# Hybrid encoder layer on one core: the mixer's value projection in 2x2 blocks, behind the block of keys and value gates

## The chip, the cores and the metric

The kernel runs on one core of a Trainium2 chip. The metric is the device time of one execution in microseconds (us), as the median of several runs. The engines are named as in the profile: PE (matrix products) with PEld (loading of its weights), DVE (vector), ACT (scalar), POOL (GpSimd) and SP (which issues most loads).

## The reference, cut to what matters

The layer is a half-step FFN, a mixer with two head groups, and a second half-step FFN, each between two norms. Width is 2048, 256 tokens, float32. What the change touches is the mixer's input projection:

```python
h = rms_norm(x, pre_norm_mix[layer])
q_h, i_h, f_fwd, f_bwd, g_h, q_a, k_a, v_a = jnp.split(h @ w_mix_in[layer], split_at, axis=-1)
y_h = hgrn2_mixer(q_h, i_h, f_fwd, f_bwd, g_h, lb_fwd_all[layer], lb_bwd_all[layer],
                  hgrn_out_norm[layer])
y_a = window_attention(q_a, k_a, v_a, attn_sink[layer], rel_bias_table)
mixed = jnp.concatenate([y_h.astype(x.dtype), y_a.astype(x.dtype)], axis=-1) @ w_mix_out[layer]
```

The columns 1024 to 2047 of `w_mix_in` give `i_h`, the values of the recurrent heads (in the kernel: `vh`). The columns 6144 to 6655 give `k_a` and `v_a`, the keys and values of the attention heads (in the kernel: `kz` and `va`). Each is a product of 256 tokens x 2048 inputs with 2048 inputs x 1024 or 512 columns.

## The kernel before, in words

**Precision.** Every product is made of three. An operand is split into a high part and a low part: ACT casts it (line 177, `h`), and DVE subtracts the cast from it (line 178, `l`). PE then adds high x high, high x low and low x high into one PSUM bank. Weights arrive by SP in chunks of 128 x 2048 (1 MB, three raw buffers), and each chunk is split in two halves of 1024 columns into h and l buffers, five of each. `xt` holds the transposed input, 16 blocks of 128 inputs, high and low, with the two halves of the tokens side by side; two neighbouring blocks are a pair, so there are eight pairs.

**A projection by 512 columns** (`proj_N`, lines 367 to 393) goes through the 16 blocks of inputs and for each half of the tokens issues three products of 128 x 512: 96 products in all, into two banks. `LeadN` (line 345) makes the first half of such a projection inside the end of the first FFN.

**The order of the mixer's start.** The values' first 512 columns, of which blocks 0 to 7 are done by `LeadN` during the FFN's last steps and blocks 8 to 15 after it; the second 512 columns; then the 512 columns of keys and gates; then the head projections (`headpair`, by `proj_T_pieces`, lines 311 to 343), whose products are lines 322 and 327. Meanwhile ACT makes the squares for the norm, POOL the power -0.5 and DVE copies the scale of each half of the tokens to `rs2` (line 264). The results are scaled on the way out of PSUM by `rs2`. `spread` (line 284) broadcasts a factor per token along the partitions, by one product on PE, into `R`; the head projections are scaled by `R`.

**Blocks with seven products.** The class `Blocks` (lines 415 to 607) is used by the FFNs and by the output projection, not by the input projection. It takes a pair of input blocks and two banks of 512 columns for each half of the tokens, a 2x2 by 2x2 block product. A plain pair takes eight block products (24 on PE). A pair that has prepared sums of `xt` (its entry in `sums`) takes seven (21 on PE), by sums on both sides. `seven` (line 476) prepares the weights of such a pair on DVE and ACT:

```python
split_act(*first, b11)
nc.vector.tensor_tensor(
    four[:, 0:2], four[:, 0::3], four[:, 1:2].to_broadcast([P, 2, 512]), ALU.add
)
lower = split_half(raw, 1)
nc.vector.tensor_tensor(b22, b11, b22, ALU.add)
upper = split_half(raw, 0)
nc.vector.tensor_tensor(b21, b22, b21, ALU.add)
last = split_half(raw, 1)
```

`products` (line 498) issues the seven on PE. Four of them go to banks of their own, and `fold` (line 526) adds these on DVE into the four result banks: four additions for the mixed sums (lines 535, 536, 539, 542) and one into each bank (548, 552, 556, 558). `play` (line 589) issues a plain pair; at the first plain pair behind the last one with sums it puts the steps of the fold between the products, and the products of the later pair add to the same banks. `sums_of` (line 406) makes the sums of `xt`: one operation of 256 columns and two of 128.

Since sums across the two halves of the tokens are only right with one scale, the first input projection of an FFN first multiplies the second half of the tokens in `xt` by the ratio of the two scales' powers of two: `power_and_rest` (line 266) makes `ratio` and `rest` in six small operations, `spread(ratio, 1)` broadcasts it, and `even` (line 1073) scales a pair (128 x 512). The results are then scaled by `rest`.

**Order.** The mixer's instructions are not in an order written by hand. A planner gives each engine its order before the run, from its own estimate of durations: of what is ready it takes what stands earliest in the program. An instruction that waits for a buffer or a result can be overtaken by later ones in the planner's order; on the chip each engine then keeps that order. The FFNs' inner parts are issued in program order (`manual_schedule`).

Of the kernel before, what the change touches and what calls it, by code (L numbers as in the profile page):

```python
# [11 lines left out]
F32 = mybir.dt.float32  # L12
F32R = mybir.dt.float32r
# [4 lines left out]
ALU = mybir.AluOpType  # L18
AX = mybir.AxisListType

P = 128
D = 2048
T = 256
DFF = 5632
KT = D // P
# [12 lines left out]
def hymba_layer_kernel(  # L38
# [25 lines left out]
    nc = tc.nc  # L64
# [11 lines left out]
    def nm(s):  # L76
        uid[0] += 1
        return f"{s}_{uid[0]}"

    def pa():  # L80
        return psum.tile([P, 512], F32, tag="pa", name=nm("pa"))
# [55 lines left out]
    R = const.tile([P, T], F32, tag="R", name="R")  # L137
# [38 lines left out]
    def split_act(hi, lo, src):  # L176
        nc.scalar.copy(hi, src)  # L177
        nc.vector.tensor_tensor(lo, src, hi.bitcast(F32), ALU.subtract)  # L178
# [62 lines left out]
    def pre_stats():  # L241
        with tc.issue_after(last["act"].ins):
            pre_stats_now()
# [22 lines left out]
    def power_and_rest():  # L266

        for part, a, b in ((two, 0x7F800000, 0), (rest, 0x007FFFFF, 0x3F800000)):
            nc.vector.tensor_scalar(
                part.bitcast(I32), rs2.bitcast(I32), a, b, ALU.bitwise_and, ALU.bitwise_or  # L270
            )
        nc.vector.tensor_scalar(
            ratio.bitcast(I32),
            two[:, 0:1].bitcast(I32),
            0x7F800000,
            0x7F800000,
            ALU.bitwise_and,
            ALU.bitwise_xor,
        )
        nc.vector.tensor_scalar(ratio, ratio, two[:, 1:2], 0.5, ALU.mult, ALU.mult)  # L280
        nc.vector.tensor_scalar(rest[:, 1:2], rest[:, 1:2], two[:, 0:1], None, ALU.mult)
        nc.vector.tensor_copy(rest[:, 0:1], rs2[:, 0:1])

    def spread(factor=rs2, n=2):

        ps = pb()
        for m in range(n):
            nc.vector.tensor_scalar(
                R[:, m * P : (m + 1) * P], ident, factor[:, m : m + 1], None, ALU.mult
            )  # L290
        nc.tensor.matmul(ps[:, : n * P], ones, R[:, : n * P], start=True, stop=True)
        nc.vector.tensor_copy(R[:, : n * P], ps[:, : n * P])
# [86 lines left out]
    def proj_N(*a, **kw):  # L379
        for _ in proj_N_pieces(*a, **kw):  # L380
            pass

    def proj_N_pieces(w, c0, n, xt, slot, k0=0):

        kn = 2048 // n
        half = kn // 2
        for kc in range(k0 // kn, KT // kn):
            hs, ls = split_load(source_N(w, c0, n, kc))
            for m in range(2):
                for kk in range(kn):  # L390
# [218 lines left out]
    class Pairs(Blocks):  # L609
# [26 lines left out]
        def source(self, u):  # L636
            return Pairs.part(self.w, u, self.now)
# [12 lines left out]
        def left_sums(self, u):  # L650
            if self.ready and u in self.ready:
                return self.ready.pop(u)
            if u in self.kept:
                return self.kept[u]
            keep = self.now == 0 and u in self.keep
            if keep and u in self.near:
                w = self.room.tile([P, 4, 2, P], F32R, tag="sp", name=nm("sp"), bufs=3)
            else:
                tag = f"sp{u}" if keep else "sp"
                w = far["pool"].tile([P, 4, 2, P], F32R, tag=tag, name=nm("sp"), bufs=1 if keep else 2)  # L660
            split_act(w[:, :, 0, :], w[:, :, 1, :], self.sums[u])
            if keep:
                self.kept[u] = w
            return w
# [240 lines left out]
    def pair_of(xt, u):  # L905
        return xt[u // 4][:, u % 4 * 2 : u % 4 * 2 + 2]

    class Gated(Blocks):


# [127 lines left out]
    def ffn(gated, w_dn, post_gain, again, gain=None, lead=None, aside=None):  # L1038

        with ExitStack() as st:  # L1040
# [31 lines left out]

            def even(u):

                x = gated.tiles[u].rearrange("p k i t -> p (k i) t")[:, :, P:T]
                nc.vector.tensor_tensor(
                    x, x.bitcast(F32), R[:, None, 0:P].to_broadcast([P, 4, P]), ALU.mult
                )

            def sums_in(u):  # L1080
                x = gated.tiles[u].bitcast(F32)
# [428 lines left out]
    def again_from(src):  # L1510
# [4 lines left out]

        return again

    vbanks = [pa(), pa()]
    xt = ffn(
        gated,  # L1520
        w_ffn1_down[0],
        post_norm_ffn1,
        again_from(x[0]),
        gain=lambda: later["cols"][:, 0:16],
        lead=LeadN(w_mix_in[0], 1024, vbanks),
        aside=other_vectors,
    )
    cols = later["cols"]
# [3 lines left out]
    with ExitStack() as s2:  # L1532
# [21 lines left out]
        def lower_bounds():  # L1554
            l0, l1 = cols[:, 32:48], cols[:, 48:64]
            nc.vector.tensor_tensor(lbm, l0, l1, ALU.max)
            nc.vector.tensor_tensor(e0, l0, lbm, ALU.subtract)
            nc.vector.tensor_tensor(e1, l1, lbm, ALU.subtract)
            nc.scalar.activation(e0, e0, AF.Exp)
            nc.scalar.activation(e1, e1, AF.Exp)  # L1560
            nc.vector.tensor_tensor(e1, e0, e1, ALU.add)
            nc.vector.reciprocal(e1, e1)
            nc.vector.tensor_tensor(lb, e0, e1, ALU.mult)
            nc.vector.tensor_scalar(oml, lb, -1.0, 1.0, ALU.mult, ALU.add)

        w_in = w_mix_in[0]
        vh = mid.tile([P, 2, 1024], F32, tag="vh", name="vh")
        for cg in range(2):
            sl = [pa(), pa()] if cg else vbanks
            if cg == 0:  # L1570
                pre_stats()
                with tc.issue_after(last["rs2"].ins):
                    lower_bounds()
            proj_N(w_in, 1024 + cg * 512, 512, xt, sl, k0=0 if cg else 8)
            for m in range(2):
                nc.scalar.mul(
                    vh[:, m, cg * 512 : (cg + 1) * 512], sl[m], rs2[:, m : m + 1]
                )


# [35 lines left out]
            return z  # L1616


        sl = [pa(), pa()]
        for i, _ in enumerate(proj_N_pieces(w_in, 6144, 512, xt, sl)):  # L1620
            if i == 16:
                spread()
        va = mid.tile([P, 2, 256], F32, tag="va", name="va")
        kz = mid.tile([P, 2, 256], F32, tag="q", name="kz")
        for m in range(2):
            nc.scalar.mul(kz[:, m, :], sl[m][:, :256], rs2[:, m : m + 1])
            nc.scalar.mul(va[:, m, :], sl[m][:, 256:], rs2[:, m : m + 1])
        kT = mid.tile([P, 2, T], F32, tag="kT", name="kT")

        def turned_keys():  # L1630
# [129 lines left out]
        def gates(half):  # L1760

            sl = [pa(), pa()]
            for _ in proj_N_pieces(w_in, 4096 + half * 512, 512, xt, sl):
                side_step()
            g = mid.tile([P, 2, 512], F32, tag="g", name=nm("g"))
            for m in range(2):
                by = rs2[:, m : m + 1]
                nc.scalar.activation(g[:, m, :], sl[m], AF.Sigmoid, scale=by)
                nc.vector.scalar_tensor_tensor(g[:, m, :], sl[m], by, g[:, m, :], ALU.mult, ALU.mult)
            return g  # L1770
# [246 lines left out]
```

## Time and profile before

| | us |
|---|---|
| median of 3 runs | 1822.63 (1822.04 to 1824.23) |
| the profiled execution's own time | 1824.3 |
| its span in the profile | 1822.5 |
| mean granted PE clock of the profiled execution | 0.999 |

The profile is of one execution. Rows of windows give a stretch of the span, its length, the busy time of each engine in it with the number of rows in brackets, the granted PE clock, the mean share of the DMA engines and GB/s. Rows of groups give line, engine, operation, output <- inputs, shape and count, then busy time and the mean duration in ns, then idle time of the engine in front of them with what ended it. Rows in order of time give start, duration, engine, line and operation, with idle time and its cause in brackets. Times of rows are us from the start of the span.

### The profile page before, as it was taken

Reading aid. Unit: us, or ns where it says so; the run is one execution under the profiler, and the core shown is the slowest. Engines: PE = TensorE matmul, PEld = TensorE weight load, DVE = VectorE, ACT = ScalarE, POOL = GpSimd, SP = SyncE. Lnnn points to the kernel's source line nnn. Section 1 sums busy time; section 2 is a strip of 40 time slices with the busy share of each in tenths; the row PEclk is TensorE's granted clock in tenths of the full one; section 3 lists DMA queues with packets and bytes.
Section 4 is the critical chain, followed back from the end, with each engine's and each line's share of the span. In section 5 each row is a group of like instructions: output and inputs, shape, how many; then the busy total and the mean of one; then the engine's idle time right before and its main releaser. Section 6 shows DMA issues by size and latency. Waiting matters only on the chain.

```text
span 1822.5 us, 23466 instructions
## 1 busy us (share of the span) xinstructions
PE 1808.9 (99%) x8420; PEld 1502.0 (82%) x8420; DVE 1605.0 (88%) x2073; ACT 1137.1 (62%) x1508; POOL 162.9 (9%) x155
## 2 busy tenths in 40 slices
PE   9999999999999999999999999999999999999998
PEld 7888888888888888888888888888888888888886
DVE  7999999999989989477687798899999999998986
ACT  7565666666666657476587556556666666566653
POOL 1011111111011100000000000111111111011110
PEclk9999999999999999999999999999999999999999
DMA  8889999998698995655454456889999999699894
GB/s 303 240 235 284 278 281 257 250 261 247 224 343 263 300 300 191 196 183 176 162 174 150 162 208 243 253 242 266 283 271 269 256 248 252 195 339 302 274 303 160
DMA packets 212052, 447.59 MB, mean 246 GB/s; under 512 B 11752, under 2 KB 46656, under 8 KB 211168
## 3 DMA queue, kind: packets, MB, share of 16 engines
q1 hardware_dynamic: 180032, 385.14, 60.7%
q0 software_dynamic: 31904, 60.96, 19.5%
q8 instruction: 66, 1.08, 0.2%
q14 instruction: 50, 0.41, 0.1%
HBM read 433.46 MB, written 12.60 MB: 245 GB/s over the span
## 4 chain that ended last, share of the span: by engine, by line
PE 86%; DVE 7%; ACT 3%; DMA 2%; issue 2%; POOL 0%; DVEq 0%; ACTq 0%; SPq 0%; POOLq 0%
PE pa L454 37%; PE pb L454 32%; PE pa L322 5%; DVE l L178 4%; PE pa L327 3%; PE pa L377 2%; PE pa L375 2%; PE pa L376 2%; DMA raw<-in_w_ffn_down_dram 2%; ACT h L177 1%; PE pa L1131 1%; PE pb L1131 1%; DMA raw<-in_w_ffn_gate_up_dram 0%; DVE la L178 0%; PE pb L1738 0%
## 5 line engine op out<-in xcount | busy, mean ns | idle before, releaser
L177 ACT CAST h<-raw 128x1024 fp32r<-128x1024 f32 (+1 forms) x867 | 854.8, 1013 | 465.3 <-PE pb L454 152.9
L178 DVE TENSOR_TENSOR l<-raw,h 128x1024 fp32r<-128x1024 f32 (+1 forms) x867 | 987.8, 1170 | 134.4 <-ACT h L177 100.6
L454 PE MATMUL pa<-h,xt 128*128 128x512 f32 x1096 | 384.9, 392 | 0.1
L454 PE MATMUL pb<-h,xt 128*128 128x512 f32 x940 | 336.7, 392 | 0.3 <-DVE pb L1188 0.3
L454 PEld LDWEIGHTS pa<-h,xt 128*128 128x128 f32 x1096 | 206.0, 188 | 44.2 <-DVE xt L233 0.6
L454 PE MATMUL pa<-l,xt 128*128 128x512 f32 x548 | 214.0, 391 | 0.0
L454 PEld LDWEIGHTS pb<-h,xt 128*128 128x128 f32 x940 | 176.5, 188 | 42.5 <-DVE pb L1195 3.6
L454 PE MATMUL pb<-l,xt 128*128 128x512 f32 x470 | 183.3, 390 | 0.0
L967 POOL DMA_DIRECT2D raw<-in_w_ffn_gate_up_dram x78 | 94.6, 1212 | 733.8 <-DVE l L178 665.8
L454 PE MATMUL pb<-h,ht 128*128 128x512 f32 x452 | 159.2, 389 | 0.0
L454 PE MATMUL pa<-h,ht 128*128 128x512 f32 x452 | 159.1, 389 | 0.0
L322 PE MATMUL pa<-xt,h 128*128 128x512 f32 x512 | 124.5, 393 | 0.2 <-ACT h L177 0.2
L454 PEld LDWEIGHTS pa<-l,xt 128*128 128x128 f32 x548 | 103.2, 188 | 20.6 <-DVE l L178 0.8
L454 PE MATMUL pa<-h,xs 128*128 128x512 f32 x312 | 111.6, 389 | 0.0
L322 PEld LDWEIGHTS pa<-xt,h 128*128 128x128 f32 x512 | 93.8, 188 | 18.7 <-ACT h L177 0.6
L454 PE MATMUL pb<-h,xs 128*128 128x512 f32 x312 | 108.7, 389 | 0.0
L454 PEld LDWEIGHTS pb<-l,xt 128*128 128x128 f32 x470 | 88.3, 188 | 16.8
L454 PEld LDWEIGHTS pb<-h,ht 128*128 128x128 f32 x452 | 84.8, 188 | 17.6
L454 PEld LDWEIGHTS pa<-h,ht 128*128 128x128 f32 x452 | 84.9, 188 | 17.5
L454 PE MATMUL pa<-l,ht 128*128 128x512 f32 x226 | 88.2, 390 | 0.9 <-DVE l L178 0.9
L454 PE MATMUL pb<-l,ht 128*128 128x512 f32 x226 | 87.9, 389 | 0.0
L1273 POOL DMA_DIRECT2D raw<-in_w_ffn_down_dram x38 | 46.0, 1212 | 374.2 <-DVE la L178 337.2
(292 smaller groups left out, 2575.6 us busy)
## 6 DMA issues: line engine op xcount, KB each, us to landing
raw<-in_w_ffn_gate_up_dram SPq DMA_DIRECT2D x350, 512.0 KB, 5.9
raw<-in_w_ffn_down_dram SPq DMA_DIRECT2D x88, 1024.0 KB, 7.8
raw<-in_w_mix_in_dram SPq DMA_DIRECT2D x52, 1024.0 KB, 5.0
raw<-in_w_ffn_gate_up_dram POOLq DMA_DIRECT2D x78, 512.0 KB, 8.1
raw<-in_w_ffn_down_dram POOLq DMA_DIRECT2D x38, 512.0 KB, 10.1
raw<-in_w_mix_out_dram SPq DMA_DIRECT2D x16, 1024.0 KB, 5.0
ht<-away SPq DMA_DIRECT2D x24, 512.0 KB, 10.3
away<-ht SPq DMA_DIRECT2D x16, 512.0 KB, 7.0
```

What stands on the lines that cost most here:

```text
L177: nc.scalar.copy(hi, src)
L178: nc.vector.tensor_tensor(lo, src, hi.bitcast(F32), ALU.subtract)
L322: nc.tensor.matmul(slot[f], weights(hs, kk, f), xcol(xt, k), start=(k == 0), stop=(k == KT - 1))
L327: nc.tensor.matmul(slot[f][:, 0:T], weights(ls, kk, f), xcol(xt, kh * 8 + kk, 0), start=False, stop=False,)
L375: nc.tensor.matmul(dst, xh, h[:, o : o + n], start=(k == 0), stop=False)
L376: nc.tensor.matmul(dst, xh, l[:, o : o + n], start=False, stop=False)
L377: nc.tensor.matmul(dst, xl, h[:, o : o + n], start=False, stop=(k == KT - 1))
L454: nc.tensor.matmul(self.bank(at), lhs, rhs, start=(n == 1), stop=n in (ends, self.of[at]), skip_group_check=n > ends,)
L967: nc.gpsimd.dma_start(raw[:, 0:1024].rearrange("p (k c) -> p k c", k=2), self.source(u, g)[:, :, 1], accum_op=ALU.add,)
L1131: nc.tensor.transpose(bank[:, o : o + P], zs[m][:, k * P : (k + 1) * P], ident)
L1273: nc.gpsimd.dma_start(raws[i][:, 0:1024].rearrange("p (k c) -> p k c", k=2), Pairs.part(w_dn, u, r)[:, :, 512:1024], accum_op=ALU.add,)
```

## The change

The block of keys and gates takes the place of the values' first 512 columns in `LeadN` and is projected first. Then all 1024 value columns are projected at once as `Blocks` (a new subclass `Values`): pairs 0, 1, 3, 6 and 7 plain, pairs 2, 4 and 5 with seven products. For that the second half of the tokens of `xt` is scaled by `ratio` in all eight pairs (`even_half`, the old body of `even` as a function), the sums of pairs 2, 4 and 5 are made (`value_sums`), and what comes after is scaled by `rest`: the values, the gates, and the head projections through `R`. The keys and gates themselves are scaled by `rs2`. The old projection of keys and gates behind the values, with `spread()` in it, is gone.

```diff
+    def even_half(x):
+
+        x = x.rearrange("p k i t -> p (k i) t")[:, :, P:T]
+        nc.vector.tensor_tensor(
+            x, x.bitcast(F32), R[:, None, 0:P].to_broadcast([P, 4, P]), ALU.mult
+        )
+
...
-    vbanks = [pa(), pa()]
+    kvbanks = [pa(), pa()]
...
-        lead=LeadN(w_mix_in[0], 1024, vbanks),
+        lead=LeadN(w_mix_in[0], 6144, kvbanks),
...
-        for cg in range(2):
-            sl = [pa(), pa()] if cg else vbanks
-            if cg == 0:
-                pre_stats()
-                with tc.issue_after(last["rs2"].ins):
-                    lower_bounds()
-            proj_N(w_in, 1024 + cg * 512, 512, xt, sl, k0=0 if cg else 8)
-            for m in range(2):
+        pre_stats()
+        with tc.issue_after(last["rs2"].ins):
+            lower_bounds()
+        power_and_rest()
+
+        class Values(Blocks):
+
+
+            def source(self, u):
+                return Pairs.part(w_in, u, 1)
+
+            def left_sums(self, u):
+                return self.sums[u]
+
+            def folded(self):
+                return [
+                    [y[:, n, :] for n in range(2)]
+                    for y in (
+                        keepy.tile([P, 2, 512], F32, tag=f"yt{4 + m}", name=nm("y"), bufs=1)
+                        for m in range(2)
+                    )
+                ]
+
+        def value_sums(u):
+
+            z, s = (keepy.tile([P, 4, P], F32, tag=f"sy{i}", name=nm("vs"), bufs=1) for i in range(2))
+            x = pair_of(xt, u).bitcast(F32)
+            whole = z.rearrange("p j t -> p (j t)").rearrange("p (k t) -> p k t", k=2)
+            nc.vector.tensor_tensor(whole, x[:, :, 0, :], x[:, :, 1, :], ALU.add)
+            w = keepy.tile([P, 4, 2, P], F32R, tag=f"yt{VALUES.index(u)}", name=nm("xs"), bufs=1)
+            split_act(w[:, :, 0, :], w[:, :, 1, :], sums_of(whole, s))
+            values.sums[u] = w
+
+        VALUES = (2, 4, 5)
+        values = Values({u: pair_of(xt, u) for u in range(KT // 2)}, dict.fromkeys(VALUES))
+        for i, _ in enumerate(proj_N_pieces(w_in, 6144, 512, xt, kvbanks, k0=8)):
+            if i == 2:
+                spread(ratio, 1)
+                for u in range(4):
+                    even_half(pair_of(xt, u))
+                value_sums(2)
+            if i == 7:
+                even_half(pair_of(xt, 4))
+                even_half(pair_of(xt, 5))
+        even_half(pair_of(xt, 6))
+        even_half(pair_of(xt, 7))
+        value_sums(4)
+        va = mid.tile([P, 2, 256], F32, tag="va", name="va")
+        kz = mid.tile([P, 2, 256], F32, tag="q", name="kz")
+        for m in range(2):
+            nc.scalar.mul(kz[:, m, :], kvbanks[m][:, :256], rs2[:, m : m + 1])
+            nc.scalar.mul(va[:, m, :], kvbanks[m][:, 256:], rs2[:, m : m + 1])
+        values.begin(range(KT // 2))
+        values.work(2)
+        value_sums(5)
+        values.work(3)
+        spread(rest)
+        values.work(KT // 2)
+        for m in range(2):
+            for n in range(2):
                 nc.scalar.mul(
-                    vh[:, m, cg * 512 : (cg + 1) * 512], sl[m], rs2[:, m : m + 1]
+                    vh[:, m, n * 512 : (n + 1) * 512], values.c[m][n], rest[:, m : m + 1]
                 )
...
-        sl = [pa(), pa()]
-        for i, _ in enumerate(proj_N_pieces(w_in, 6144, 512, xt, sl)):
-            if i == 16:
-                spread()
-        va = mid.tile([P, 2, 256], F32, tag="va", name="va")
-        kz = mid.tile([P, 2, 256], F32, tag="q", name="kz")
-        for m in range(2):
-            nc.scalar.mul(kz[:, m, :], sl[m][:, :256], rs2[:, m : m + 1])
-            nc.scalar.mul(va[:, m, :], sl[m][:, 256:], rs2[:, m : m + 1])
...
-                by = rs2[:, m : m + 1]
+                by = rest[:, m : m + 1]
```

More of the change, by code (lines that the diff above doesn't have):

```diff
@@ L1073, in even @@
             def even(u):
[L1075 to L1078, printed above, removed]
+                even_half(gated.tiles[u])
             def sums_in(u):
```

## The prediction

> **What bounds the kernel now.** I read the page's totals and its chain first, then the stretch that the change touches, by windows, by groups and in order of time.
>
> ```profile
> PE 1808.9 (99%) x8420; PEld 1502.0 (82%) x8420; DVE 1605.0 (88%) x2073; ACT 1137.1 (62%) x1508; POOL 162.9 (9%) x155
> PE 86%; DVE 7%; ACT 3%; DMA 2%; issue 2%; POOL 0%; DVEq 0%; ACTq 0%; SPq 0%; POOLq 0%
> 718.70:729.60 10.90, 10.90 (x49) 9.01 (x48) 9.49 (x26) 9.63 (x21) 1.10 (x2) 1.00 0.87 282
> 729.60:773.50 43.90, 43.90 (x195) 36.36 (x194) 20.50 (x21) 20.49 (x22) 0.00 (x0) 1.00 0.61 198
> L375 PE MATMUL pa<-h,xt 128*128 128x512 f32 x64 | 25.1, 392 | 0.0
> L376 PE MATMUL pa<-l,xt 128*128 128x512 f32 x64 | 24.9, 389 | 0.0
> L377 PE MATMUL pa<-h,xt 128*128 128x512 f32 x64 | 24.9, 389 | 0.0
> L178 DVE TENSOR_TENSOR l<-raw,h 128x1024 fp32r<-128x1024 f32 x17 | 20.7, 1225 | 23.3 <-ACT h L177 22.7
> L177 ACT CAST h<-raw 128x1024 fp32r<-128x1024 f32 x17 | 17.8, 1052 | 19.5 <-PE pa L377 19.5
> ```
>
> The window rows give length, then busy time of PE, weight loads, DVE, ACT and POOL, the granted clock, the DMA share and GB/s. PE carries 86% of the chain, so a product saved counts fully where PE is the engine that is late. The second window is the stretch in question: from 729.6 us (the first 512 value columns are done) to 773.5 (the second value block and the block of keys and value gates are done). There 192 products of 128x512 run without a gap. Their listed 0.39 us overlap; the step is (43.9 - 0.43 for one broadcast) / 192 = 0.226 us. DVE is busy 20.5 of 43.9 us and waits for ACT's casts, which wait for PE to give back h buffers: the weights are always ready early. But one window earlier DVE is busy 9.5 of 10.9 us. DVE has room only inside the second window, 23.4 us of it, and the change spends it.
>
> **The change on PE.** The three 512-column blocks need 288 products, the new form 96 + 5 x 24 + 3 x 21 = 279. Keys and gates take the first place, half of it inside the FFN's end as before, so 729.6 stays the start and 183 products follow instead of 192. That is 9 x 0.226 = 2.0 us saved. One broadcast becomes two:
>
> ```profile
> 726.10 1.23 DVE L178 TENSOR_TENSOR l<-raw,h 128x1024 fp32r<-128x1024 f32 x1 [0.21 <-ACT h L177]
> 762.88 0.43 PE pb L291 x2
> 1143.96 0.15 DVE L264 COPY scales<-r 128x1 f32<-128x1 f32 x1 [0.73 <-POOL r L187]
> 1145.86 0.29 DVE L288 TENSOR_SCALAR R<-ident,scales 128x128 f32<-128x128 f32 x1
> 1153.11 0.29 DVE L292 COPY R<-pb 128x128 f32<-128x128 f32 x1
> 1153.43 2.50 DVE L1076 TENSOR_TENSOR xt<-xt,R 128x512 fp32r<-128x512 f32 x4
> 731.26 2.36 DVE L178 TENSOR_TENSOR l<-raw,h 128x1024 fp32r<-128x1024 f32 x2 [1.14 <-ACT h L177]
> 764.46 0.42 DVE L292 COPY R<-pb 128x256 f32<-128x256 f32 x1
> 728.05 0.15 DVE L264 COPY scales<-r 128x1 f32<-128x1 f32 x1 [0.47 <-POOL r L187]
> 728.12 0.17 DVE L1556 TENSOR_TENSOR lbm<-cols 128x16 f32<-128x16 f32 x1
> ...
> 729.94 0.18 DVE L1564 TENSOR_SCALAR oml<-lb 128x16 f32<-128x16 f32 x1
> ```
>
> The second row is the broadcast of two halves; the new one has one half, 0.2 us. PE's net gain is 1.8 us, and that is all the change can gain: the stretch has no PE gap that could vanish.
>
> [...]
>
> **The change on DVE.** Durations overlap here too. Four scalings by R (L1076) take 2.50 us, and one takes 0.69, so the step is (2.50 - 0.69)/3 = 0.60 us for 512 columns; two splits take 2.36 with 1.22 for one, so 1.14 for 1024. The same in smaller sizes: 256 columns listed at 0.42 step 0.34, 128 columns listed at 0.29 step 0.20 (estimates, the list value less the same 0.08).
>
> ```profile
> 1157.05 0.42 DVE L408 TENSOR_TENSOR s<-z 128x256 f32<-128x256 f32 x1
> L411 DVE TENSOR_TENSOR sums<-sums,z 128x128 f32<-128x128 f32 x16 | 4.7, 292 | 0.5
> L1083 DVE TENSOR_TENSOR z<-xt 128x512 f32<-128x512 f32 x8 | 5.5, 684 | 0.0
> L178 DVE TENSOR_TENSOR xs<-s,xs 128x512 fp32r<-128x512 f32 x8 | 5.5, 687 | 2.3 <-ACT xs L177 2.2
> L486 DVE TENSOR_TENSOR raw<-raw 128x1024 f32<-128x1024 f32 x4 | 4.9, 1219 | 0.0
> L490 DVE TENSOR_TENSOR raw<-raw 128x512 f32<-128x512 f32 x4 | 2.8, 688 | 0.1
> L548 DVE TENSOR_TENSOR pa<-pa,y 128x512 f32<-128x512 f32 x6 | 4.1, 688 | 0.0
> ```
>
> All new operations stand in the trace of other stages. Counted from 728.05, where the second half's scale lands and the ratio can first be made:
> - power_and_rest, six small operations: from 1143.96 to 1145.86 with one split of 1.14 between, so 0.7 us; lower_bounds as before, seven of 0.17 to 0.25 between its two rows above, about 1.1.
> - spread(ratio): 0.2 for the factor (L288) and 0.2 for the copy (L292); spread(rest): two factors and the copy of both halves, 0.9, as before.
> - even_half, eight times 0.60: 4.8.
> - value_sums, three times 0.60 + 0.34 + 0.20 + 0.20 + 0.60: 5.8.
> - plain pairs 1, 3, 6, 7, two splits each: 8 x 1.14 = 9.1. Pair 0 is split before 728, as the chunk in its place was (the row at 726.10).
> - seven-product pairs 2, 4, 5: a first block 0.60, the double sum (L486) 1.14, two sums 1.20, three splits 3.42, so 6.36 each: 19.1. A plain pair costs 2.28. Three products of 0.226 saved on PE cost 4.1 us of DVE.
> - the fold, eight additions (L535 to L558, one of them shown): 4.8.
>
> The sum is 46.7 us. Where the added time goes: DVE had 20.5 us of work in the stretch and gets about 45 in it.
>
> **What is late next.** DVE takes what stands earlier in the program and is ready. It can begin even_half at about 730.9 (an estimate: 728.1, then 0.7 for power_and_rest, 0.2 for the factor, some 1.3 for the products already under way and the broadcast on PE, 0.2 for the copy, and the hand-overs). The eight even_half and the opening of value_sums(2), 6.2 us, stand ahead of pair 1's splits, so its first low part is there at 738.2; PE, with pair 0 alone (24 x 0.226 and the broadcast from 729.6), runs dry at 735.2. That is 3.0 us idle. The planner can pull pair 3's and later pair 6's products into later gaps, as they need no sums, but not further: every one needs DVE's splits, and the first block of each seven-product pair already waits on DVE. So the end is DVE's queue. Pair 7 comes last: its splits stand behind the last splits of pair 5 and the fold, and its products behind the fold's additions to the same banks. DVE waits itself for the pass of R, for ACT's casts and for the copy that opens the fold:
>
> ```profile
> 1049.20 1.23 DVE L178 TENSOR_TENSOR l<-raw,h 128x1024 fp32r<-128x1024 f32 x1 [0.22 <-ACT h L177]
> 1053.02 1.23 DVE L178 TENSOR_TENSOR l<-raw,h 128x1024 fp32r<-128x1024 f32 x1 [0.26 <-ACT h L177]
> 1059.39 1.23 DVE L178 TENSOR_TENSOR l<-raw,h 128x1024 fp32r<-128x1024 f32 x1 [0.53 <-ACT h L177]
> ```
>
> These are the waits of 1045 to 1060, where the mixer's output projection splits two such pairs: 1.0 us in 15. Over 47 us that is 3; with DVE this full ACT is less often the late one, and I take 2.3. Then DVE is through with pair 7 at 728.05 + 46.7 + 2.3 = 777.1, its first half 1.14 earlier at 775.9, and PE needs 24 x 0.226 = 5.4 us from there: 781.3. Before, the stretch ended at 773.5. The sum is +7.8 us.
>
> Bounds. Below: no waits on DVE, and pair 7's splits ahead of the fold, so that only six products stand behind DVE's last addition: 774.8 + 1.4 = 776.2, +2.7; steps 3 per cent shorter take another 1.4 us, so +1.3. Above: every DVE operation at its listed duration, as if each depended on the one before. Two that do start 0.73 us apart:
>
> ```profile
> 1175.26 0.69 DVE L981 TENSOR_TENSOR raw<-raw 128x512 f32<-128x512 f32 x1
> 1175.99 0.69 DVE L982 TENSOR_TENSOR raw<-raw 128x512 f32<-128x512 f32 x1
> ```
>
> That adds 0.08 to 31 operations of 512 columns, 20 of 1024 and some 20 small ones, 5.7 us in all: +13.5.
>
> The fold reads PSUM, and its 688 ns (L548) are those of the same size in SBUF (L490). [...]
>
> **What else moves, at no cost.** ACT keeps 17 casts of 1024 columns in the stretch (nine for the seven-product pairs, eight for plain ones) and gets six of 512 and one copy of that size, 0.62 each by the row below: 20.5 + 4.3 = 24.8 us of 43.9. If it were late, its casts would stand in DVE's way, and the upper bound is the price. SP issues the same 1 MB loads, now as 4 KB rows (DMA share 0.61). No queue has a bias or store moved past it. POOL keeps its two powers. After 781 the head stage runs as before: its first products (L322) follow the stretch at once, and DVE is busy 5.7 of 11.3 us there, so its queue is empty within one projection and nothing is won back or lost.
>
> ```profile
> L177 ACT CAST xs<-s 128x512 fp32r<-128x512 f32 x8 | 5.0, 619 | 13.3 <-DVE s L412 13.2
> 773.37 1.98 PE L322 MATMUL pa<-xt,h 128*128 128x512 f32 x8
> 773.50:784.80 11.30, 11.30 (x69) 10.07 (x68) 5.73 (x5) 5.53 (x7) 0.00 (x0) 1.00 0.57 186
> ```
>
> **Rivals.** Forecast A: DVE is the bound of the values; +4 to +12. For it: 46.7 us of work against 43.
>
> B, not slower: DVE keeps ahead and only PE's count changes, -1.8 us (1820.8). Its place is the last split of pair 5. If that lands before PE has used up pairs 0 to 5, about 759, all stays hidden. Some 37 us of queue stand before it from 728, so six of them would have to vanish. For it: the two halves of the output projection run the same code at full PE speed,
>
> ```profile
> 1040.00:1050.00 10.00, 10.00 (x46) 8.28 (x45) 9.70 (x12) 6.09 (x7) 0.00 (x0) 1.00 0.24 81
> 1050.00:1060.00 10.00, 10.00 (x46) 8.29 (x45) 9.21 (x11) 6.60 (x8) 0.00 (x0) 1.00 0.49 183
> ```
>
> with DVE at 9.2 to 9.7 of 10. Against it: there a plain pair stands between the two and no scaling of xt is needed, and DVE has no reserve even so.
>
> C: the planner fills better than I do, and gaps are partly closed by the first head projection or by pairs 3, 6 and 7 brought forward: 0 to +4, 1824.6 in the middle. Against it: all of these pass through the same DVE queue.
>
> D: DVE's operations mostly follow one that they depend on, as in the upper bound, and full raw or h buffers add waits for the next load: beyond +12, some 1836.
>
> **How the numbers follow.** A 0.68, B 0.10, C 0.12, D 0.10. The profiled execution took 1824.3 us with a span of 1822.5; +7.8 there is 1832.1. The median of the runs is 1822.63, 1.7 below it, so I forecast 1830.4. The range for 8 in 10: from +1.3 (below it lie B and a little of C) to +14 (above it the end of D), so 1824 to 1837. A measurement of this kernel tells some 0.2% from no change, 3.6 us. Slower by more: A, D and 0.01 of C, 0.79. Within: the rest of C and half of B, 0.16. Faster by more than that needs a gain twice PE's own, from a place that I don't see: half of B, 0.05.
>
> **What would show it.** Right: weight loads, 8.28 of 10 us wherever PE runs full, drop to 6 or 7 between 735 and 781, with PE's waits naming DVE's l, xs and raw; DVE above 9 of 10 from 728 to 777; the first gap at about 735, 3 us long; the first head projection starting at about 781. Wrong: weight loads at 8.28 throughout and the head projection at 771 or 772 (B); gaps that ACT or the loads end (then the price has another owner); or a later stage that moves by more than the stretch does.

## The result, and the profile after

The changed kernel takes 1828.71 us (median of 5 runs, 1828.16 to 1829.94) against 1822.63 before (median of 5 runs, the three of the table ahead and two more): a ratio of 1.0033, with a 95% interval from 1.0022 to 1.0045, or 6.1 us more (4.0 to 8.2). The profiled execution has a span of 1826.9 us at a mean granted clock of 0.996.

The page's totals and its chain, as shown of before:

```profile
PE 1809.9 (99%) x8413; PEld 1500.4 (82%) x8413; DVE 1631.9 (89%) x2127; ACT 1142.4 (63%) x1518; POOL 162.9 (9%) x155
PE 91%; DVE 4%; ACT 3%; DMA 1%; issue 1%; SPq 0%; POOL 0%; DVEq 0%; ACTq 0%; POOLq 0%
```

DVE has 54 operations and 26.9 us more. PE has seven rows fewer: nine products less, two for the second broadcast more. The totals can't say where it hurts, so the windows of the stretch come next, each row with its length, busy PE, weight loads, DVE, ACT and POOL, clock, DMA share and GB/s:

```profile
730.00:740.00 10.00, 10.00 (x46) 8.12 (x44) 10.00 (x21) 2.48 (x4) 0.00 (x0) 1.00 0.09 12
740.00:750.00 10.00, 7.79 (x23) 4.78 (x22) 9.21 (x16) 5.76 (x8) 0.00 (x0) 0.78 0.32 105
750.00:760.00 10.00, 10.00 (x40) 8.16 (x39) 9.57 (x11) 4.52 (x5) 0.00 (x0) 0.88 0.63 219
760.00:770.00 10.00, 9.52 (x41) 7.26 (x40) 8.47 (x9) 6.27 (x7) 0.00 (x0) 1.00 0.35 129
770.00:780.00 10.00, 10.00 (x46) 8.27 (x45) 10.00 (x14) 5.41 (x7) 0.00 (x0) 1.00 0.79 262
...
726.83:776.00 49.17, 45.93 (x183) 35.17 (x182) 45.81 (x79) 23.82 (x30) 0.00 (x0) 0.93 0.43 146
```

DVE is busy 8.5 to 10 of every 10 us, where before it was busy 20.5 of 43.9. The last row runs from the arrival of the second scale to the end of pair 7's last split: 49.2 us, of which DVE works 45.8. PE's idle time lies in two windows, 740 to 750 and 760 to 770. Besides, its granted clock is below 1.00 from 740 to 760: in the window from 750 PE is busy throughout, with 40 rows in place of 46. In order of time on PE, with idle time and its cause in brackets:

```profile
728.22 0.49 PE L291 MATMUL pb<-R,ones 128*128 128x128 f32 x2 [0.56 <-DVE R L288]
...
744.95 0.50 PE L454 MATMUL pa<-l,xs 128*128 128x512 f32 x1 [1.80 <-DVE l L178]
...
746.91 0.80 PE L454 MATMUL pb<-h,xs 128*128 128x512 f32 x1 [0.37 <-ACT h L177]
...
757.97 0.39 PE L454 MATMUL pa<-h,xs 128*128 128x512 f32 x1
...
762.73 0.39 PE L454 MATMUL pa<-h,xs 128*128 128x512 f32 x1
...
763.84 0.50 PE L454 MATMUL pa<-h,xs 128*128 128x512 f32 x1 [0.26 <-ACT h L177]
...
764.78 0.72 PE L454 MATMUL pa<-h,xt 128*128 128x512 f32 x2 [0.21 <-ACT h L177]
...
778.99 3.33 PE L322 MATMUL pa<-xt,h 128*128 128x512 f32 x14
```

The waits are, but for the last, those of the seven-product pairs: the inputs `xs` are the sums of xt. 744.95 and 746.91 belong to pair 2; pair 4's sums are first read at 757.97 and pair 5's at 762.73, and 763.84 is pair 5's. 764.78 belongs to a plain pair behind it, pair 6 by the program's order: pair 5's own six products of `xt` into `pa` are done before 762.73. From 764.8 on PE runs full to the head projection. DVE's rows around the same places:

```profile
726.81 0.15 DVE L264 COPY scales<-r 128x1 f32<-128x1 f32 x1 [0.66 <-POOL r L187]
...
736.79 1.22 DVE L178 TENSOR_TENSOR l<-raw,h 128x1024 fp32r<-128x1024 f32 x1
...
741.54 0.68 DVE L1600 TENSOR_TENSOR vs<-xt 128x512 f32<-128x512 f32 x1
742.14 0.68 DVE L178 TENSOR_TENSOR xs<-vs,xs 128x512 fp32r<-128x512 f32 x1
742.75 0.68 DVE L490 TENSOR_TENSOR raw<-raw 128x512 f32<-128x512 f32 x1
743.35 0.41 DVE L408 TENSOR_TENSOR vs<-vs 128x256 f32<-128x256 f32 x1
743.68 1.21 DVE L178 TENSOR_TENSOR l<-raw,h 128x1024 fp32r<-128x1024 f32 x1
...
763.81 4.63 DVE L178 TENSOR_TENSOR l<-raw,h 128x1024 fp32r<-128x1024 f32 x4 [1.37 <-ACT h L177]
...
769.14 1.22 DVE L178 TENSOR_TENSOR l<-raw,h 128x1024 fp32r<-128x1024 f32 x1
...
774.79 5.76 DVE L178 TENSOR_TENSOR l<-raw,h 128x1024 fp32r<-128x1024 f32 x5
```

The low part that PE waits for at 744.95 is made at 743.68, and ahead of it stand sums of xt for pairs 4 and 5 (L1600, L408, and L178 into `xs`), which PE reads 13 and 18 us later. DVE never idles between 736.79 and 743.68: it works on the wrong thing, or on too much. Between the last two rows lies the fold. The wait at 746.91 is put down to ACT, but ACT's cast had itself waited for DVE, for the sum of L492:

```profile
745.81 1.04 ACT L177 CAST h<-raw 128x1024 fp32r<-128x1024 f32 x1 [3.85 <-DVE raw L492]
```

A clean measure of the stretch needs no absolute times: from the second scale's arrival (L264) to the first long run of the head projection (L322). Before: 773.37 - 728.05 = 45.3 us. After: 778.99 - 726.81 = 52.2, or 6.4 more when the two head products are counted that the planner pulled ahead into the stretch (0.45 us). That is as much as the 6.1 us of the medians. The two profiled spans differ by 4.4 us only, because the execution of before was 1.7 us above its median; its second scale came 1.2 us later than that of the changed kernel. The experiments below use the same measure and call it the stretch.

### The profile page after: what moved, and what is told of

Same layout as the page of the kernel before. It is cut to its first block, busy times and chain, and to the rows that moved or that the text cites. A ratio compares the mean times of both kernels' runs of the same rounds, so it can differ in the third digit from the quotient of the medians.

```text
span 1826.9 us, 23524 instructions
## 1 busy us (share of the span) xinstructions
PE 1809.9 (99%) x8413; PEld 1500.4 (82%) x8413; DVE 1631.9 (89%) x2127; ACT 1142.4 (63%) x1518; POOL 162.9 (9%) x155
## 4 chain that ended last, share of the span: by engine, by line
PE 91%; DVE 4%; ACT 3%; DMA 1%; issue 1%; SPq 0%; POOL 0%; DVEq 0%; ACTq 0%; POOLq 0%
PE pa L454 41%; PE pb L454 36%; PE pa L322 5%; PE pa L327 3%; DVE l L178 2%; DMA raw<-in_w_ffn_gate_up_dram 1%; ACT h L177 1%; PE pa L377 1%; PE pa L376 1%; PE pa L375 1%; PE pa L1135 1%; PE pb L1135 1%; PE pb L1785 0%; PE pb L1759 0%; PE pb L1863 0%
## 5 line engine op out<-in xcount | busy, mean ns | idle before, releaser
L178 DVE TENSOR_TENSOR l<-raw,h 128x1024 fp32r<-128x1024 f32 (+1 forms) x873 | 992.3, 1168 | 112.5 <-ACT h L177 82.7
L454 PE MATMUL pa<-h,xt 128*128 128x512 f32 x1148 | 403.4, 392 | 0.4 <-ACT h L177 0.2
L454 PE MATMUL pb<-h,xt 128*128 128x512 f32 x986 | 353.8, 393 | 0.3 <-DVE pb L1192 0.3
L454 PEld LDWEIGHTS pa<-h,xt 128*128 128x128 f32 x1148 | 215.9, 188 | 46.9 <-ACT h L177 0.6
L454 PE MATMUL pa<-l,xt 128*128 128x512 f32 x574 | 224.5, 391 | 0.5 <-DVE l L178 0.4
L454 PEld LDWEIGHTS pb<-h,xt 128*128 128x128 f32 x986 | 185.7, 188 | 44.7 <-DVE pb L1199 3.8
L454 PE MATMUL pb<-l,xt 128*128 128x512 f32 x493 | 192.4, 390 | 0.0
L454 PEld LDWEIGHTS pa<-l,xt 128*128 128x128 f32 x574 | 108.1, 188 | 22.6 <-DVE l L178 1.5
L322 PE MATMUL pa<-xt,h 128*128 128x512 f32 x512 | 124.6, 393 | 0.2 <-ACT h L177 0.2
L454 PE MATMUL pa<-h,xs 128*128 128x512 f32 x324 | 116.3, 390 | 0.3 <-ACT h L177 0.3
L454 PE MATMUL pb<-h,xs 128*128 128x512 f32 x324 | 114.0, 392 | 0.4 <-ACT h L177 0.4
L322 PEld LDWEIGHTS pa<-xt,h 128*128 128x128 f32 x512 | 93.8, 188 | 18.7 <-ACT h L177 0.6
```

The source lines that it names most:

```text
L322: nc.tensor.matmul(slot[f], weights(hs, kk, f), xcol(xt, k), start=(k == 0), stop=(k == KT - 1))
L454: nc.tensor.matmul(self.bank(at), lhs, rhs, start=(n == 1), stop=n in (ends, self.of[at]), skip_group_check=n > ends,)
```

## The experiments

T1: the length of DVE's queue sets the end of the values. T2: one gap ahead of pair 2's products, and a slow clock behind it (below), are the price. T3: ACT, late loads or raw buffers held too long are. Kernels that were compared together share their runs of before, whose medians lie between 1822.8 and 1823.2 us.

### The move alone, and the scalings alone

`e1_plain_all` keeps the new order but makes all pairs plain, with no scaling; `e2_plain_even` adds the scalings and both broadcasts.

Both:

```diff
-        VALUES = (2, 4, 5)
+        VALUES = ()
...
-                value_sums(2)
...
-        value_sums(4)
...
-        value_sums(5)
```

e1 besides, where the values, the gates and `R` take `rs2` again in place of `rest`:

```diff
-        power_and_rest()
...
-                spread(ratio, 1)
-                for u in range(4):
-                    even_half(pair_of(xt, u))
...
-                even_half(pair_of(xt, 4))
-                even_half(pair_of(xt, 5))
-        even_half(pair_of(xt, 6))
-        even_half(pair_of(xt, 7))
...
-        spread(rest)
+        spread()
```

> The moved order alone: keys and gates first, then the values as plain 2x2 blocks, no scaling by the ratio, no sums, no fold. PE has the 192 products of before behind 729.6, DVE 20.5 us of work in 44. Both theories: within 1 us of before, 1822 to 1824, no PE gap over 0.5 us in the stretch, granted clock 1.00. If it is 3 us slower or more, the move and the wide blocks are to blame, and neither the sevens nor the clock.

> The moved order with the eight scalings by the ratio and the two broadcasts, but all pairs plain. DVE gets 4.8 + 0.7 us more than in the plain form. Both theories: hidden but for PE's wait for the factor of the broadcast (0.6 us in the changed kernel) and the broadcast itself (0.2): 1823 to 1824.5. If it is near the changed kernel (1828.7), the scalings at the start are the whole price.

Measured: e1 1822.7 us, ratio 0.9999 (0.999 to 1.0007); e2 1824.28, ratio 1.0006 (0.9997 to 1.0015). The start and the end of the stretch in e1, one row each from DVE's and PE's timeline:

```profile
727.40 0.15 DVE L264 COPY scales<-r 128x1 f32<-128x1 f32 x1 [0.47 <-POOL r L187]
...
772.75 0.62 PE L322 MATMUL pa<-xt,h 128*128 128x512 f32 x2
```

And in e2:

```profile
726.39 0.15 DVE L264 COPY scales<-r 128x1 f32<-128x1 f32 x1 [0.66 <-POOL r L187]
...
727.80 0.49 PE L291 MATMUL pb<-R,ones 128*128 128x128 f32 x2 [0.60 <-DVE R L288]
...
772.82 3.79 PE L322 MATMUL pa<-xt,h 128*128 128x512 f32 x16
```

The stretch is 45.35 us in e1, as before, and 46.43 in e2. The move costs nothing. The scalings cost 1.1 us, and PE shows where most of it is: at the broadcast of the ratio, for which it waits 0.60 us. The eight scalings themselves are hidden (PE has no other wait); e2's whole time can't be told from before.

### Filling the gap

`e3_fill_gap` puts eight products of 128x512, whose result nothing reads, ahead of the late one.

```diff
+            def products(self, u, first, lower, upper, last, order=range(7)):
+                parts = first, lower, upper, last
+                super().products(u, *parts, range(3))
+                for _ in range(8 if u == 2 else 0):
+                    nc.tensor.matmul(self.p[3], scanm[:, 0:P], scanm, start=True, stop=True)
+                super().products(u, *parts, range(3, 7))
```

> The changed kernel with eight extra products of 128x512 on PE in pair 2, between its third and fourth block product, into the bank of p7 before that is begun: they add 1.8 us of PE work where PE stood still for 1.8 to 2.0 us, and DVE's work stays. Theory 1 (DVE's queue sets the end, the slow clock only fills time in which PE would have waited): the clock stays at 1.00, PE waits later instead, 1828 to 1829. Theory 2 (one DVE gap of 2 us and 6.8 us at half clock behind it are the price): the clock stays at 1.00 and 3 us come back, 1825 to 1826.

Measured: 1828.33 us, ratio 1.0028 (1.0017 to 1.0039). One window of e3:

```profile
740.00:750.00 10.00, 8.35 (x35) 5.10 (x35) 9.21 (x15) 5.46 (x7) 0.00 (x0) 1.00 0.32 105
```

And PE's waits in e3, in order of time:

```profile
745.25 0.50 PE L454 MATMUL pa<-l,xs 128*128 128x512 f32 x1 [0.29 <-DVE l L178]
...
747.21 0.50 PE L454 MATMUL pb<-h,xs 128*128 128x512 f32 x1 [0.76 <-ACT h L177]
...
748.47 0.50 PE L454 MATMUL pb<-l,xs 128*128 128x512 f32 x1 [0.53 <-DVE l L178]
...
773.07 0.74 PE L322 MATMUL pa<-xt,h 128*128 128x512 f32 x2 [0.53 <-ACT h L177]
```

The gap is nearly closed and the clock stays at 1.00, yet the time is that of the changed kernel within its interval. PE only meets the next late operand sooner: 0.76 and 0.53 us at places where it had waited 0.37 or not at all. Against T2, and for T1.

### The scalings on POOL

`e4_even_pool` makes the mixer's eight scalings on POOL; the FFN's stay on DVE.

```diff
-    def even_half(x):
+    def even_half(x, engine=nc.gpsimd):
...
-        nc.vector.tensor_tensor(
+        engine.tensor_tensor(
             x, x.bitcast(F32), R[:, None, 0:P].to_broadcast([P, 4, P]), ALU.mult
         )
...
-                even_half(gated.tiles[u])
+                even_half(gated.tiles[u], nc.vector)
```

> The changed kernel with the mixer's eight scalings on POOL, which idles there: DVE loses 4.8 us of queue ahead of pair 1 and pair 2. Theory 1: up to 4.8 us back, 1824 to 1825.5. Theory 2: the gap at 743 goes and with it the slow clock, 5 us or more back, 1822 to 1824. If POOL needs over 1.4 us for one scaling, PE waits for POOL instead and the time is 1826 or more.

Measured: 1831.1 us, ratio 1.0044 (1.0031 to 1.0056). The group of the scalings on POOL:

```profile
L911 POOL TENSOR_TENSOR xt<-xt,R 128x512 fp32r<-128x512 f32 x8 | 13.1, 1677 | 2.4 <-PE pa L376 2.4
```

Two of DVE's groups beside it (window 728.5 to 743), with busy time and mean ns:

```profile
L486 DVE TENSOR_TENSOR raw<-raw 128x1024 f32<-128x1024 f32 x1 | 2.3, 2305 | 0.0
...
L1600 DVE TENSOR_TENSOR vs<-xt 128x512 f32<-128x512 f32 x1 | 1.8, 1765 | 1.2 <-POOL xt L911 1.2
```

A scaling takes 1.68 us on POOL against 0.68 on DVE, so the expectation's last condition (over 1.4 us for one) is met. DVE waits 1.2 us for the first pairs, and seven of its own operations beside POOL's are 0.9 to 1.1 us longer each: 2.31 us for L486, which takes 1.22 in the changed kernel, and 1.77 for L1600 against 0.68 at 741.54 there. The seven together are 7.4 us longer, and the eight scalings that DVE is rid of were 4.8. So DVE's queue got some 2.6 us longer and not shorter, and the time is 2.4 us above the changed kernel's. Theory 1's number failed on POOL's price; the direction is that of T1.

### More work on DVE, more on ACT

`e5_dve_more` and `e6_act_more` add one copy to each seven-product pair, on the one engine or the other (`nc.scalar.copy` in e6).

```diff
             )
+            self.more(raw)
             lower = split_half(raw, 1)
...
+            def more(self, raw):
+                nc.vector.tensor_copy(vh[:, 0, :], raw[:, 0:1024])
```

> Each of the three seven-product pairs gets one more DVE operation of 128x1024, a copy of the finished double sum into a buffer that nothing reads: 3 x 1.14 = 3.4 us of DVE work between 735 and 770, nothing else. T1 (DVE's queue sets the end of the values): nearly all of it shows, +2.5 to +3.5 on the changed kernel's 1828.5, so 1831 to 1832. T2 (one gap and the clock behind it are the price): DVE had a few us to spare behind the gap, so at most +1, 1828.5 to 1829.5. T3 (ACT or late loads set the end): 0 to +1.

> The same copy on ACT: 3 x 1.05 = 3.2 us of ACT work at the same three places, DVE's as in the changed kernel. T1: ACT is busy about 25 of the 50 us, but DVE waits for its casts, so a part shows: 0 to +1.5, 1828.5 to 1830. T3 (ACT's casts set the end): +2.5 to +3.2, 1831 to 1832.

Measured: e5 1830.3 us, ratio 1.0041 (1.0028 to 1.0054); e6 1828.92, ratio 1.0036 (1.0024 to 1.0049). The copies of e5 cost DVE less than was expected, as its timeline shows:

```profile
740.11 0.68 DVE L1588 COPY vh<-raw 128x1024 f32<-128x1024 f32 x1
```

The next operation starts at 740.71, so a copy of 1024 columns takes a step of 0.60 us and not the 1.14 of a sum of that size: 1.8 us were added on DVE, not 3.4. Of these, 1.6 show in the median; of 3.2 on ACT (three copies of 1.05 us) 0.2. That is as T1 has it, and the misses of its numbers lie in the price of the copy. But both intervals overlap the changed kernel's, so these two runs alone decide nothing. One window of e6:

```profile
740.00:750.00 10.00, 7.25 (x27) 4.41 (x26) 9.21 (x15) 5.91 (x8) 0.00 (x0) 1.00 0.30 104
```

In this profile the clock never fell, with no filling, and the time is the same as with 6.8 us of half clock. That too speaks against T2.

### Less work on DVE

`e7_no_sums` leaves out all three sums over the weights, `e12_no_double` the double one alone. The diff is e7's; its last lines stand in `Values`, and the FFNs and the output projection keep their sums.

```diff
+            add = self.add
-            nc.vector.tensor_tensor(
+            add(
                 four[:, 0:2], four[:, 0::3], four[:, 1:2].to_broadcast([P, 2, 512]), ALU.add
             )
             lower = split_half(raw, 1)
-            nc.vector.tensor_tensor(b22, b11, b22, ALU.add)
+            add(b22, b11, b22, ALU.add)
             upper = split_half(raw, 0)
-            nc.vector.tensor_tensor(b21, b22, b21, ALU.add)
+            add(b21, b22, b21, ALU.add)
...
+            def add(self, *of):
+                pass
```

> The seven-product pairs keep their splits, their 21 products, the sums of xt and the fold, but leave out the three sums over the weights on DVE (the double one and two single ones). DVE's queue is 3 x (1.14 + 0.60 + 0.60) = 7.0 us shorter. T1: the queue then ends before PE does, and PE's own count remains: 9 products fewer, one broadcast more and what the scalings cost (+1.3 at most): 1821 to 1823.5. T2: the gap in front of pair 2's products loses 1.1 to 1.8 us, the slow clock with it: also about 1824. T3 (the loads are late because a raw buffer is held over a whole seven): each buffer is free about 2 us earlier, but the next load still takes its time: 1825 to 1827.

> Only the double sum over the weights of the seven-product pairs is left out, and no load takes its place; the two single sums stay. DVE's queue is 3.4 us shorter, and ACT's casts need not wait for it. T1 (DVE's queue sets the end, and the adding load of the two runs before cost its own latency): half of what leaving out all three sums gave, 1824.5 to 1826.5. T5 (below a certain length of the queue the pairs are no longer late one after the other, and nothing of the price remains): 1822.5 to 1824. If the DVE work hardly matters: 1827.5 or more.

Measured: e7 1822.71 us, ratio 0.9999 (0.999 to 1.0007); e12 1825.78, ratio 1.0017 (1.0008 to 1.0026). The stretch of e7, from DVE's and PE's timeline:

```profile
726.84 0.15 DVE L264 COPY scales<-r 128x1 f32<-128x1 f32 x1
...
728.18 0.49 PE L291 MATMUL pb<-R,ones 128*128 128x128 f32 x2 [0.61 <-DVE R L288]
...
771.41 3.79 PE L322 MATMUL pa<-xt,h 128*128 128x512 f32 x16
```

With 7.0 us less on DVE the price is gone, although the seven-product pairs, their products, the sums of xt and the fold are all there. With 3.4 less, 2.9 us are won, and one larger gap is left:

```profile
744.81 0.50 PE L454 MATMUL pb<-h,xs 128*128 128x512 f32 x1 [1.49 <-ACT h L177]
```

DVE's work taken off comes back almost one for one in the medians: 6.0 of 7.0 us, 2.9 of 3.4. The interval of e7 lies wholly below the changed kernel's; e12's overlaps its lower end, but all eleven runs of e12 are faster than the five of the changed kernel. T3 expected something else in e7, and T5, a price that vanishes at once, in e12. On T2 the two runs say little, as its forecast for e7 was near T1's. Both also shorten the chain of steps within a pair, since ACT's casts no longer wait for the sums. That this chain and not the sum of DVE's work is the price is what e6 speaks against: its copies stand in the same chain, on ACT, ahead of the cast of the double sum, and cost 0.2 us.

### Two seven-product pairs, spaced

```diff
-        VALUES = (2, 4, 5)
+        VALUES = (3, 6)
...
-                value_sums(2)
+                value_sums(3)
...
-        value_sums(4)
...
-        value_sums(5)
+        value_sums(6)
```

> Seven products in pairs 3 and 6 alone, spaced, pair 5 plain again: 282 products in place of 279. DVE loses a seven against a plain pair, 4.1 us, and one set of sums, 1.9: 40.7 us in place of 46.7. T1: DVE ends at about 771, at the time of PE's own end: before -1.2 to +1.5, 1821.5 to 1824.5. A theory T4 that the price is one of the seven's machinery as such (the fold, the banks of their own, the order of the products) and not of the sum of DVE's work: a third less of the sums but the same fold, 1826 to 1828.

Measured: 1823.22 us, ratio 1.0001 (0.9992 to 1.001). Its windows where the changed kernel lost time:

```profile
740.00:750.00 10.00, 10.00 (x45) 8.28 (x45) 9.93 (x16) 4.49 (x5) 0.00 (x0) 1.00 0.62 211
...
760.00:770.00 10.00, 10.00 (x46) 8.29 (x45) 8.72 (x9) 6.49 (x7) 0.00 (x0) 1.00 0.40 131
```

PE runs full with the same fold, so the machinery as such (T4) is not the price. Two things differ from the changed kernel at once, the number of such pairs and their spacing; which of them does more was not tried. Of the versions with seven-product pairs that compute the layer it is the nearest to before, but it is no gain.

### The order of the sums, and an adding load

`e9_late_sums` makes the sums of pairs 4 and 5 later; `e10_dma_double` makes the double sum over the weights by a load that adds; `e11_dma_late` does both. First the order (e9, e11), then the load in place of L486 (e10, e11):

```diff
-        value_sums(4)
...
         values.begin(range(KT // 2))
-        values.work(2)
+        values.work(3)
+        value_sums(4)
+        spread(rest)
+        values.work(4)
         value_sums(5)
-        values.work(3)
-        spread(rest)
```

```diff
+            def double(self, u, four):
+                nc.gpsimd.dma_start(
+                    four[:, 0:2], self.source(u)[:, :, 512:1024], accum_op=ALU.add
+                )
```

> The sums of xt for pair 4 are made behind pair 3 in the program, and those for pair 5 behind pair 4, in place of both ahead of pair 2's and 3's splits. DVE's work is the same to the operation, only its order changes: 1.9 us of it no longer stand ahead of pair 2's splits. T1 (the length of DVE's queue sets the end): the gap at 744.9 shrinks and comes back behind; 1827 to 1829. T2 (that one gap, and the clock behind it, are the price): both go, 1.8 and up to 3.4 us, 1823 to 1826.5.

> The double sum over the weights of a seven-product pair (1.14 us of DVE, three times) is made by an adding load from DRAM, queued by POOL, in place of DVE; what is computed is the same. DVE's queue is 3.4 us shorter, but each pair waits for a load inside its chain (the 1 MB loads land some 5 us after they are issued) and holds its raw buffer longer. T1: DVE's work decides, 1824 to 1826. T3 (latency and the raw buffers decide): no gain or a loss, 1828 to 1832.

> Both together: the adding load, and the later sums of xt. T1: DVE's queue is 3.4 us shorter as in the run before, and the order adds little: 1823 to 1826. T2: the gap ahead of pair 2's products goes with the order of the sums: 1822 to 1824. T3: 1828 or more.

Measured: e9 1828.46 us, ratio 1.0027 (1.0017 to 1.0038); e10 1842.7, ratio 1.0106 (1.0092 to 1.012); e11 1839.9, ratio 1.0093 (1.0078 to 1.0109). PE's waits in e9:

```profile
744.10 0.50 PE L454 MATMUL pb<-h,xs 128*128 128x512 f32 x1 [0.56 <-ACT h L177]
...
756.57 0.50 PE L454 MATMUL pb<-h,xs 128*128 128x512 f32 x1 [0.92 <-ACT h L177]
...
761.83 0.50 PE L454 MATMUL pa<-h,xs 128*128 128x512 f32 x1 [0.97 <-ACT h L177]
```

With the same DVE work in a better order the 1.8 us gap is gone, and the time with it is not: the waits come back 12 and 17 us later. T2 is out as the main cause. It may hold a part: with the head products taken off, the stretches of e3 (727.12 to 778.23), e6 (727.62 to 779.01) and e9 (726.42 to 776.97), where the clock stayed at 1.00, are 50.7, 51.2 and 50.1 us against 51.7 of the changed kernel. That is 0.6 to 1.6 us in single traces, while the medians differ by 0.4 at most.

In e10 T1's forecast failed by some 17 us, and T3's by 11; in e11 only T3's, which had no upper end, held. The waits of e10's stretch, who waited for whom, us in total, times and the longest:

```profile
ACT h L177 <- DMA raw<-in_w_mix_in_dram: 18.4, 4, 9.4
DVE raw L488 <- DMA raw<-in_w_mix_in_dram: 16.8, 3, 7.3
```

And e10's loads from 735 to 790, with the engine that issues, count, KB of each and median us to landing:

```profile
raw<-in_w_mix_in_dram POOLq DMA_DIRECT2D x3, 512.0 KB, 7.1
```

The adding load lands 7.1 us after its issue. The chain of a pair (first split, sum, splits) waits for it, and ACT's and DVE's orders wait behind that chain. e12 took the same 3.4 us off DVE without that load and won 2.9, so it is the load that costs the rest, through the waits above. That T1 holds only while each pair's chain is shorter than the time that DVE spends on other work is my reading of this; no run measures where the limit lies.

## Why the prediction was right

The direction, the cause and the range were right: DVE is the bound of the values, the forecast's own case (+4 to +12) came out with +6.1, where +7.8 was forecast.

DVE's queue. Predicted: 46.7 us of work and 2.3 of waits, 49.0 from the second scale to pair 7's last split. Measured: 49.2, with 45.8 busy and 3.4 idle. Two small errors cancel: pair 1's first half was already split before the scale arrived (-1.1), and the waits were longer (+1.1). The longest is the 1.37 us at 763.81. ACT's timeline shows why it comes:

```profile
762.25 0.59 ACT L541 COPY y<-pa 128x512 f32<-128x512 f32 x1 [3.65 <-PE pa L454]
762.73 5.79 ACT L177 CAST h<-raw 128x1024 fp32r<-128x1024 f32 x6
```

The copy that opens the fold stands ahead of pair 5's casts and waits 3.65 us for PE's product of the same pair. So in this stretch a late PE made ACT late (3.65 us), ACT made DVE late (1.37 at 763.81), and DVE PE (1.80 at 744.95).

The steps of the queue. In the window from 728 to 780:

```profile
L178 DVE TENSOR_TENSOR l<-raw,h 128x1024 fp32r<-128x1024 f32 x20 | 23.7, 1218 | 2.5 <-ACT h L177 2.5
L911 DVE TENSOR_TENSOR xt<-xt,R 128x512 fp32r<-128x512 f32 x8 | 5.4, 676 | 0.0
```

Single operations last as listed (676 and 1218 ns), and in a full queue their starts lie closer: 0.60 us between the rows at 741.54, 742.14 and 742.75. The steps that were taken from other stages hold here, and the upper bound by listed durations did not come near.

What is late next. The first gap was put at 735 and 3.0 us long; it came ahead of 744.95 with 1.8. Pair 1's first half being split early, PE had 36 products and not 24 from 729.25, enough until 737.4, and the second half of pair 1 was there at 738.0. The wait moved on to pair 2. This step named the right queue and the wrong place in it, and the end did not depend on it.

The end: the term that was too large. I put all of pair 7 behind the fold, so 4.3 us of PE time behind DVE's last split (24 products from 775.9, against a last split at 777.1). In the planner's order its first half stands ahead of most of the fold (769.14) and only the second behind it (774.79). PE had other products in between, even two of the head's, and was 3.0 us from the end when DVE was through at 776.0. The last operands that PE waits for are those at 764.78, of the plain pair behind pair 5, not pair 7's. These 1.3 us, with the 0.45 of the two head products and less the 0.2 by which the queue was longer and 0.1 of rounding, are the difference between +7.8 and the 6.4 of the stretch.

PE's saving. 1.8 us were counted, 0.8 are there: e7, with PE never late, has a stretch of 44.57 against 45.32. The products bring nearly the 2.0 that was said (from the first product of the values to the head projection 42.21 us, against 43.97 in e1: 1.76). But the ratio's broadcast was priced at 0.2 us of PE time, and PE also waits 0.6 for it. Rival B at its best would have been -0.8 and not -1.8, too little to be measured. It did come out, once DVE was 7.0 us shorter: its condition, six of 37 us gone, lies between the 3.4 of e12, which were not enough, and the 7.0 of e7, which were.

Rivals C and D: the planner did fill (pair 1, pair 7, two head products), which moved the gaps and took the last term down by 1.3 us; D's chains of dependent operations showed little (L492 starts 0.73 us behind L490 in pairs 4 and 5, in place of 0.60), and its late loads only in e10 and e11. Whether a fourth raw buffer would help was not tried.

What would show it: weight loads fell, to 4.8 and 7.3 of 10 in two windows and not throughout; DVE was above 9 of 10 in four windows of five; the head projection began at 779.0 in a trace whose second scale came 1.2 us early, 780.2 on the scale of the forecast, against 781. Not as said: PE's waits were to name DVE, and gaps that ACT ends were put down as a sign of another owner. DVE ends the longest, 1.80 us, and ACT's casts the other three behind 740, 0.84 us together. One of these casts had waited for DVE (745.81), another for the copy that opens the fold (762.25), and more work on ACT cost 0.2 us in e6; so the price has the owner that was named, by way of ACT too.

## What to carry to other kernels

Before products are traded for sums on another engine, add up that engine's work between the first moment it can start and the last operand that PE needs: here, by count, 41 us with two spaced pairs were hidden under 44 us of PE, and 47 with three cost 6. When PE shows a gap, ask whether the queue behind it is too long or only badly ordered: filling or moving the gap gave 0.4 us at most, and shortening the queue gave nearly all of what was taken off it (6.0 us of 7.0, 2.9 of 3.4). Work taken off a busy engine was no gain where its replacement put a latency into each item's chain: in e10 loads that landed 7.1 us after their issue took 3.4 us, by count, off DVE, and the time was 1842.7 us against 1828.71.

## What the runs showed of the hardware

The granted clock fell after short gaps, and not each time. In the changed kernel PE had run full for over 10 us, waited 1.80 us, and then was granted half its clock for 6.8 us:

```profile
745.50:752.30 6.80, 6.39 (x15) 4.10 (x14) 6.01 (x9) 4.93 (x6) 0.00 (x0) 0.50 0.43 143
```

In e5, after gaps of 0.65, 1.46 and 0.76 us between 742 and 747, it fell for some three:

```profile
747.00:751.00 4.00, 3.67 (x8) 2.44 (x9) 3.80 (x4) 4.00 (x6) 0.00 (x0) 0.57 0.38 88
```

In e6 gaps of 1.33, 0.76, 0.53 and 1.66 us left it at 1.00. So one gap of 1.80 us, and three of 1.46 at most, had the half clock behind them, and four of up to 1.66 had not; what decides it, no run here tests. In these runs, with DVE the bound, the half clock cost little: e3, e6 and e9, without it in their profiles, have medians within 0.4 us of the changed kernel's. Nor did the time follow the clock among the changed kernel's own runs: 1828.71 and 1829.55 us at a mean clock of 0.996, 1828.66 and 1829.94 at 0.998.

Beside POOL's scalings (eight in 13.15 us) most of DVE's operations were slower. Seven took 0.9 to 1.1 us longer, as the rows of e4 show for two; one, a split at 731.85, took its usual 1.21. Why the seven were longer and the split was not, no run shows.
